# Expert layer of a two-block network on one core: a fourth weight buffer, sums of the dense part kept in `h`, gathered sums in the tile of `x`, gate tiles in another pool, stores on ScalarE's queue

## The chip, the cores and the metric

The kernel runs on one core of a Trainium2 chip. The metric is the device time of one execution in microseconds, as the median of several runs. The change concerns the expert layer (called `peer` in the code), but two of its edits resize buffer pools that all layers share.

## What is computed

A block with a hybrid mixer and an expert layer, then a second block with a pooling layer and a sparse attention layer, on 256 tokens of width 2048. The expert layer picks, for every token, 8 heads x 16 experts out of 16384, and each expert is one row of `expert_down` and one of `expert_up`:

```python
def block(args):
    xb, idx, gb = args
    u = expert_down[idx]
    act = jax.nn.gelu(jnp.einsum('thkd,td->thk', u, xb), approximate=False)
    vv = expert_up[idx]
    return jnp.einsum('thk,thkd->td', (gb * act).astype(vv.dtype), vv)
```

## The kernel before

**Weights.** Every large matrix comes in tiles of 1 MB (128 x 2048 fp32). `split_w` (L149) takes a buffer `wr` from a pool of three, lets SyncE (SP) issue the load, and then splits each half of the tile: ScalarE rounds it to `wh` (L159), VectorE subtracts to get the rest `wl` (L161). TensorE multiplies with both parts. A buffer `wr` is free again when the second `wl` has been made; SP issues the load into it at that time, in the order of its own queue. The weights of the second block's modulation (`in_mod_w`, L1008) use the same three buffers and are worked on by VectorE alone (L1014).

**The expert layer does tokens in two ways.** Tokens 0 to 191 go through all 16384 experts densely: 128 weight tiles of `in_down`, the activation (GELU), a multiplication with a table of gates that is zero for experts that were not picked, and 128 weight tiles of `in_up`. Tokens 192 to 255 go by gathers: GpSimd (POOL) fetches, slot by slot, the 128 rows (1 MB) that the 64 tokens need, by an indirect DMA into a tile `fm` (L772); VectorE multiplies and sums such a row tile with the tile of `x` (`x2`, L780) for `down_rows`, and multiplies it with the slot's activation and adds it to `acc` (L795) for `up_rows`. There are 64 gathers for each. `fm` has seven buffers, of which three hold the packed input `hx` of the dense part.

**Order.** The code runs over 16 panels of experts. `down(c)` takes four tiles and `up(p)` eight. The first 18 `down` stand alone; then `up` of a panel and two `down` take turns, and the last `up` stand alone. Results of the first seven panels (`LAG = 7`) are stored to DRAM (`hidden`, L843) and loaded again in `prep` (L856). `step()` is called after each weight tile and advances the gathers by `PUMP = 0.57`. The list scheduler that comes after the recording decides each engine's order from priorities and from buffers that it sees as free, so pools move work.

**Gate table.** `gate_table` builds, in 24 blocks, the gates of 8 tokens at a time out of one-hot tiles `A`, `B` in pool `s4` (L746, VectorE), multiplies them on TensorE (L732), collects 16 tokens in a tile of pool `gl` (L735, ScalarE) and stores it to DRAM (L738, SP). `prep` loads the gates of a panel into one `fm` tile (L860), multiplies (L865) and splits the result (L868, L869).

**Pool `gl`** has six buffers of 8 KB per partition. In the expert layer it holds `x2`, the sums `acc` of `up` for tokens 128 to 191 (their hi parts in partitions 0 to 63, their lo parts in 64 to 127, folded at the end by a product with `ff`, L897), the gathered sums `acc` (L785), activations and the split operands of `up`. `h` holds the 256 tokens' stream in two halves of 128 partitions; the rows 64 to 127 of its second half are the 64 gathered tokens.

Of the kernel before, what the change touches and what calls it, by code (L numbers as in the profile page):

```python
# [10 lines left out]
F32 = mybir.dt.float32  # L11
# [11 lines left out]
D = 2048  # L23
# [14 lines left out]
class Kern:  # L38
    def __init__(self, tc, ctx, d):
        self.tc, self.nc, self.d = tc, tc.nc, d  # L40
        pool = lambda name, bufs, **kw: ctx.enter_context(tc.tile_pool(name=name, bufs=bufs, **kw))
        self.cst = self.ph = pool("cst", 1)
        self.wr = pool("wr", 3)
        self.whp = pool("wh", 3)
        self.wlp = pool("wl", 3)
        self.fmp = pool("fm", 7)
        self.gl = pool("gl", 6)
        self.s4 = pool("s4", 4)
        self.s2 = pool("s2", 4)
        self.sm = pool("sm", 2)  # L50
        self.k1 = pool("k1", 4)
        self.mdp = pool("md", 1)
        self.accp = pool("acc", 4, space=PSUM)
        self.trp = pool("tr", 2, space=PSUM)
        self.msp = pool("ms", 2, space=PSUM)
        self.cnt = 0
        self.consts()
        self.mods = self.mod_steps()
        self.posts, self.seq, self.bg_rate, self.bg_due, self.nmods = [], [], 0.0, 0.0, 0
        self.pump, self.credit = None, 0.0  # L60
# [650 lines left out]
    def gate_table(self, R, G):  # L711
# [11 lines left out]
        def products(n, A, B):  # L723
# [13 lines left out]
            if n % GT == GT - 8:  # L737
                nc.sync.dma_start(G[n // GT], st)  # L738

# [13 lines left out]

    def gathers(self, h, R, inv, x2, ff):

# [28 lines left out]
        nc.vector.tensor_tensor(act, act, gt, op=OP.mult)  # L784
        acc = self.t_gl([128, D])  # L785
        for j in range(66):
            if j < 64:
                issue("up_rows", j)
            if j >= 2:
                r = rows.pop(j - 2)  # L790
                c = act[:, j - 2:j - 1]
                if j == 2:
                    nc.vector.tensor_scalar(acc, r, c, None, op0=OP.mult)
                else:
                    nc.vector.scalar_tensor_tensor(acc, r, c, acc, op0=OP.mult, op1=OP.add)  # L795
            yield
        for dc in range(4):
            cs = slice(dc * 512, (dc + 1) * 512)
            p = self.p_ms()
            nc.tensor.matmul(p, ff[:, 0:128], acc[:, cs], start=True, stop=True)  # L800
            nc.vector.tensor_tensor(h[:, 1, cs], h[:, 1, cs], p, op=OP.add)
            yield

    def peer(self, h):
# [18 lines left out]
        S = self.tc.dram_tile([LAG, 128, 8, TD], F32, name="hidden")  # L823
        C, act = {}, {}

        def down_post(c, tm):
# [15 lines left out]
            if i < LAG:  # L842
                nc.sync.dma_start(S[i, :, 4 * q:4 * q + 4], dst)  # L843

# [8 lines left out]
        def prep(p):  # L853
# [3 lines left out]
            else:  # L857
                a = act.pop(p)
            g8 = self.t_fm([128, TD // GT, 8, GT], F32)
            nc.sync.dma_start(g8, G[:, :, 8 * p:8 * p + 8, :].rearrange("g p i t -> p g i t"))  # L860
            c0, cp = self.t_gl([128, 2, 8, 128], F32R), self.t_s4([128, 8, 128], F32R)
            for q in range(2):
                s = slice(4 * q, 4 * q + 4)
                a4 = a[:, s].rearrange("p i (g t) -> p g i t", t=GT)
                nc.vector.tensor_tensor(a4, a4, g8[:, :, s], op=OP.mult)  # L865
                for hi, lo, src in ((c0[:, 0, s], c0[:, 1, s], a[:, s, 0:128]),
                                    (cp[:, s, 0:64], cp[:, s, 64:128], a[:, s, 128:TD])):
                    nc.scalar.activation(hi, src, AF.Copy)  # L868
                    nc.vector.tensor_tensor(lo, src, hi.bitcast(F32), op=OP.subtract)  # L869
            C[p] = c0, cp  # L870

        ss = self.ss_mod(0)
        acc = None
        ups = [*range(LAG, 15), 0, 15, *range(1, LAG)]

        def up(p):
            nonlocal acc
            if p == ups[0]:
                acc = self.t_gl([128, D])
            c0, cp = C.pop(p)  # L880
            xs = [(c0[:, 0, e], c0[:, 1, e], cp[:, e]) for e in range(8)]
            for dc in range(4):
# [5 lines left out]
                with self.first(end):  # L888
                    s = h[:, 0, cs]
                    nc.vector.tensor_tensor(s, s, ps[0], op=OP.add)  # L890
                    if p == ups[0]:
                        nc.vector.tensor_copy(acc[:, cs], ps[1])
                    else:
                        nc.vector.tensor_tensor(acc[:, cs], acc[:, cs], ps[1], op=OP.add)
                    if p == ups[-1]:
                        q = self.p_ms()
                        nc.tensor.matmul(q, ff[:, 64:192], acc[:, cs], start=True, stop=True)  # L897
                        nc.vector.tensor_tensor(h[:, 1, cs], h[:, 1, cs], q, op=OP.add)
                        for t in range(2):
# [13 lines left out]
        for c in range(4):  # L913
# [6 lines left out]
            if c == 0:  # L920
                nc.vector.scalar_tensor_tensor(x2[64:128], h[64:128, 1], inv[64:128, 1:2], x2[64:128],
                                               op0=OP.mult, op1=OP.mult)
                nc.scalar.dma_start(x2[0:64], x2[64:128])

        def start():
            yield
            self.pump = self.gathers(h, R, inv, x2, ff)
            next(self.pump)
# [574 lines left out]
```

## Time and profile before

| what | value |
|---|---|
| time, three runs | 2772.51, 2777.41, 2774.01 us |
| median | 2774.01 us |
| profiled execution, its own time | 2777.65 us |
| its span on the core | 2775.9 us |
| granted TensorE clock, mean | 0.983 |
| busy: TensorE 2642.5, VectorE 2244.1, ScalarE 1394.2, GpSimd 271.3 us | 95%, 81%, 50%, 10% of the span |
| read from HBM, written | 759.11 MB, 20.23 MB |

The profile is of one execution, whose own time is 3.6 us above the median and 1.75 us longer than its span. Matmuls overlap, so a share of busy time near 100% does not mean that TensorE is at its peak; how many matmuls it ran in a stretch tells more. "DMA share" is the mean busy share of the core's 16 DMA engines. The chain that ended last is followed back from the last instruction and says, for each piece of time, which work the end was waiting for.

### The profile page before, as it was taken

The numbers are of one execution on the slowest core, as the hardware profiler recorded it, in microseconds if no ns is written. First come the engines' busy times: TensorE is split into PE (matmuls) and PEld (weight loads), VectorE is DVE, ScalarE is ACT, GpSimd is POOL, SyncE is SP. The second block draws the span as 40 slices with busy tenths as digits, with TensorE's granted clock in tenths as the row PEclk, the third lists the DMA queues.
The fourth block names the chain that finished last, engine by engine and source line by source line (L and its number), as shares of the span: only waits on it lengthen the run. The fifth ranks groups of instructions, "written<-read, shape, count | busy, mean of one in ns | idle before, by whom it ended". The sixth has DMA issues, their size and how long they took to land.

```text
span 2775.9 us, 33244 instructions
## 1 busy us (share of the span) xinstructions
PE 2642.5 (95%) x12296; PEld 2142.0 (77%) x12296; DVE 2244.1 (81%) x3162; ACT 1394.2 (50%) x1881; POOL 271.3 (10%) x210
## 2 busy tenths in 40 slices
PE   8999999998998999999999899998999799999998
PEld 6787778877876777787877677777887687888886
DVE  6988886999997898768998789967779867765655
ACT  5547555554654444454544444444444444455543
POOL 1000000001112222102322212000000000000000
PEclk9999999999999999999999999999999899999999
DMA  7666675557999999869999999765788855655554
GB/s 291 261 224 227 259 261 203 195 202 265 382 374 398 358 372 373 320 238 334 406 366 374 353 363 357 291 224 219 277 304 324 310 201 193 226 208 187 182 194 170
DMA packets 135123, 782.08 MB, mean 282 GB/s; under 512 B 14000, under 2 KB 38736, under 8 KB 43760
## 3 DMA queue, kind: packets, MB, share of 16 engines
q1 hardware_dynamic: 113680, 639.81, 62.4%
q0 software_dynamic: 20752, 138.53, 12.8%
q8 instruction: 96, 1.57, 0.2%
q10 hardware_dynamic: 528, 1.61, 0.2%
q14 instruction: 67, 0.55, 0.1%
HBM read 759.11 MB, written 20.23 MB: 281 GB/s over the span
## 4 chain that ended last, share of the span: by engine, by line
PE 64%; DVE 14%; DMA 13%; issue 4%; ACT 3%; POOL 0%; ACTq 0%; DVEq 0%; POOLq 0%; SPq 0%
PE acc L170 16%; PE acc L171 16%; PE acc L169 16%; DVE wl L161 6%; PE acc L219 5%; PE acc L220 5%; DMA wr<-in_down 4%; DMA wr<-in_up 4%; ACT wh L159 2%; DMA wr<-in_mod_w 2%; DVE md L1014 1%; PE tr L267 1%; DVE gl L795 1%; DVE fm L780 1%; DMA wr<-in_pool_w_out 1%
## 5 line engine op out<-in xcount | busy, mean ns | idle before, releaser
L159 ACT ACTIVATE wh<-wr 128x1024 fp32r<-128x1024 f32 x944 | 991.4, 1058 | 1127.1 <-PE acc L171 380.7
L161 DVE TENSOR_TENSOR wl<-wr,wh 128x1024 fp32r<-128x1024 f32 x944 | 1140.5, 1220 | 408.2 <-ACT wh L159 398.9
L170 PE MATMUL acc<-wl,fm 128*128 128x512 f32 x1952 | 775.0, 397 | 29.5 <-DVE wl L161 28.7
L169 PE MATMUL acc<-wh,fm 128*128 128x512 f32 x1952 | 780.6, 402 | 16.4 <-ACT wh L159 14.4
L171 PE MATMUL acc<-wh,fm 128*128 128x512 f32 x1952 | 768.3, 394 | 0.0
L170 PEld LDWEIGHTS acc<-wl,fm 128*128 128x128 f32 x1952 | 370.5, 190 | 124.1 <-DVE wl L161 50.7
L169 PEld LDWEIGHTS acc<-wh,fm 128*128 128x128 f32 x1952 | 369.5, 190 | 95.5 <-ACT wh L159 18.8
L171 PEld LDWEIGHTS acc<-wh,fm 128*128 128x128 f32 x1952 | 370.1, 190 | 75.0
L170 PE MATMUL acc<-wl,gl 128*128 128x512 f32 x768 | 307.9, 401 | 18.6 <-DVE wl L161 18.6
L169 PE MATMUL acc<-wh,gl 128*128 128x512 f32 x768 | 305.2, 398 | 10.6 <-ACT wh L159 9.4
L171 PE MATMUL acc<-wh,gl 128*128 128x512 f32 x768 | 302.6, 394 | 0.0
L1014 DVE SCALAR_TENSOR_TENSOR md<-wr,c_c,md 128x1024 f32<-128x1024 f32 x180 | 230.4, 1280 | 35.4 <-DMA wr<-in_mod_w 33.4
L219 PE MATMUL acc<-wh,s 128*128 128x512 f32 x512 | 202.8, 396 | 0.0
L220 PE MATMUL acc<-wl,s 128*128 128x512 f32 x512 | 202.7, 396 | 0.0
L219 PE MATMUL acc<-wh,fm 128*128 128x512 f32 x512 | 202.2, 395 | 0.0
L220 PE MATMUL acc<-wl,fm 128*128 128x512 f32 x512 | 202.0, 395 | 0.0
L170 PEld LDWEIGHTS acc<-wl,gl 128*128 128x128 f32 x768 | 145.2, 189 | 63.9 <-DVE wl L161 31.8
L169 PEld LDWEIGHTS acc<-wh,gl 128*128 128x128 f32 x768 | 145.0, 189 | 46.0 <-ACT wh L159 12.2
L772 POOL DMA_INDIRECT fm<-in_up_rows,slot_rows x64 | 124.0, 1938 | 482.1 <-DVE gl L795 257.0
L171 PEld LDWEIGHTS acc<-wh,gl 128*128 128x128 f32 x768 | 145.5, 189 | 31.7 <-issue 1.0
L795 DVE SCALAR_TENSOR_TENSOR gl<-fm,slot_act,gl 128x2048 f32<-128x2048 f32 x63 | 147.7, 2344 | 6.1 <-DMA fm<-in_up_rows,slot_rows 6.1
L780 DVE SCALAR_TENSOR_TENSOR fm<-fm,gl 128x2048 f32<-128x2048 f32 x64 | 146.1, 2284 | 0.2 <-DMA fm<-in_down_rows,slot_rows 0.2
(416 smaller groups left out, 2377.6 us busy)
## 6 DMA issues: line engine op xcount, KB each, us to landing
wr<-in_down SPq DMA_DIRECT2D x128, 1024.0 KB, 8.6
wr<-in_up SPq DMA_DIRECT2D x128, 1024.0 KB, 8.1
wr<-in_mod_w SPq DMA_DIRECT2D x96, 1024.0 KB, 5.2
wr<-in_attn_w_in SPq DMA_DIRECT2D x72, 1024.0 KB, 4.8
wr<-in_w_in SPq DMA_DIRECT2D x44, 1024.0 KB, 5.2
wr<-in_pool_w_in SPq DMA_DIRECT2D x32, 1024.0 KB, 5.3
wr<-in_w_out SPq DMA_DIRECT2D x16, 1024.0 KB, 4.8
wr<-in_peer_query SPq DMA_DIRECT2D x16, 1024.0 KB, 4.7
```

Source lines behind the costliest of these rows:

```text
L159: nc.scalar.activation(wh, wr[:, s], AF.Copy)
L161: nc.vector.tensor_tensor(wl, wr[:, s], wh.bitcast(F32), op=OP.subtract)
L169: mm(ps, xl, wh, start=first, stop=False)
L170: mm(ps, xh, wl, start=False, stop=False)
L171: mm(ps, xh, wh, start=False, stop=last)
L219: mm(ps[1], xp, h, start=st, stop=False)
L220: mm(ps[1], xp, l, start=False, stop=sp)
L267: self.nc.tensor.transpose(p[:, j, t * 128:(t + 1) * 128], src(t, k + j), self.ident)
L772: nc.gpsimd.indirect_dma_start(rows[j], None, d[src], bass.IndirectOffsetOnAxis(ap=ei[:, j:j + 1], axis=0))
L780: nc.vector.scalar_tensor_tensor(r, r, 1.0, x2, op0=OP.mult, op1=OP.mult, accum_out=act[:, j - 2:j - 1])
L795: nc.vector.scalar_tensor_tensor(acc, r, c, acc, op0=OP.mult, op1=OP.add)
L1014: nc.vector.scalar_tensor_tensor(acc, w[:, j], cd[:, k:k + 1], acc, op0=OP.mult, op1=OP.add)
```

## The change

- Pool `wr` gets four buffers in place of three; pool `gl` five in place of six.
- The second sum of `up` goes into `h[:, 1]` itself. For that, rows 64 to 127 of `h[:, 1]` (the gathered tokens) are stored to a DRAM tile `h_last` early on and set to zero, and at the end they are loaded into a `gl` tile `last`, whose other half is zero; the gathered sums are added to `last`, and the fold adds `last` too. The separate `gl` tile for the sum of `up` is gone.
- The gathered sums of `up_rows` go into `x2`, which is no longer needed once the last `down_rows` has been multiplied.
- The gates of a panel come by two DMAs into two `s4` tiles, in place of one DMA into one `fm` tile.
- The stores of the gate table and of `hidden` are issued by ScalarE (ACT) and not by SP.

```diff
-        self.wr = pool("wr", 3)
+        self.wr = pool("wr", 4)
...
-        self.gl = pool("gl", 6)
+        self.gl = pool("gl", 5)
...
             if n % GT == GT - 8:
-                nc.sync.dma_start(G[n // GT], st)
+                nc.scalar.dma_start(G[n // GT], st)
...
-    def gathers(self, h, R, inv, x2, ff):
+    def gathers(self, R, x2, ff, last):
...
-        acc = self.t_gl([128, D])
+        acc = x2
...
+        last.append(self.t_gl([128, D]))
+        nc.gpsimd.memset(last[0][0:64], 0.0)
+        nc.sync.dma_start(last[0][64:128], self.h_last)
         for dc in range(4):
...
             nc.tensor.matmul(p, ff[:, 0:128], acc[:, cs], start=True, stop=True)
-            nc.vector.tensor_tensor(h[:, 1, cs], h[:, 1, cs], p, op=OP.add)
+            nc.vector.tensor_tensor(last[0][:, cs], last[0][:, cs], p, op=OP.add)
...
             if i < LAG:
-                nc.sync.dma_start(S[i, :, 4 * q:4 * q + 4], dst)
+                nc.scalar.dma_start(S[i, :, 4 * q:4 * q + 4], dst)
...
-            g8 = self.t_fm([128, TD // GT, 8, GT], F32)
-            nc.sync.dma_start(g8, G[:, :, 8 * p:8 * p + 8, :].rearrange("g p i t -> p g i t"))
+            g8 = [self.t_s4([128, TD // GT, 4, GT]) for _ in range(2)]
+            for q in range(2):
+                i = 8 * p + 4 * q
+                nc.sync.dma_start(g8[q], G[:, :, i:i + 4, :].rearrange("g p i t -> p g i t"))
...
-                nc.vector.tensor_tensor(a4, a4, g8[:, :, s], op=OP.mult)
+                nc.vector.tensor_tensor(a4, a4, g8[q], op=OP.mult)
...
-                    s = h[:, 0, cs]
-                    nc.vector.tensor_tensor(s, s, ps[0], op=OP.add)
-                    if p == ups[0]:
-                        nc.vector.tensor_copy(acc[:, cs], ps[1])
-                    else:
-                        nc.vector.tensor_tensor(acc[:, cs], acc[:, cs], ps[1], op=OP.add)
+                    for t in range(2):
+                        s = h[:, t, cs]
+                        nc.vector.tensor_tensor(s, s, ps[t], op=OP.add)
                     if p == ups[-1]:
                         q = self.p_ms()
-                        nc.tensor.matmul(q, ff[:, 64:192], acc[:, cs], start=True, stop=True)
-                        nc.vector.tensor_tensor(h[:, 1, cs], h[:, 1, cs], q, op=OP.add)
+                        nc.tensor.matmul(q, ff[:, 64:192], h[:, 1, cs], start=True, stop=True)
+                        nc.vector.tensor_tensor(h[:, 1, cs], last[0][:, cs], q, op=OP.add)
...
                 nc.scalar.dma_start(x2[0:64], x2[64:128])
+                nc.scalar.dma_start(self.h_last, h[64:128, 1])
+                nc.gpsimd.memset(h[64:128, 1], 0.0)
```

The order of instructions moves at two places that matter here. The first is SP's queue where the gate table is made. Before, stores (`hidden`, `gates`) stand between the loads of weights:

```order
L154 DMA wr_5937<-in_down 128x2048
L843 DMA hidden<-s_1096_5626 128x768
L154 DMA wr_6000<-in_down 128x2048
L154 DMA wr_6060<-in_down 128x2048
L843 DMA hidden<-s_1138_5836 128x768
L738 DMA gates<-gl_5782 128x2048
L154 DMA wr_6134<-in_down 128x2048
```

Of the change, SP has nothing but loads of weights there, 48 of `in_down` in a row, and the two kinds of store stand in ScalarE's queue, behind the activations that write their tiles:

```order
L159 ACTIVATE wh_5942<-wr_5940 128x1024
L845 ACTIVATE s_1138_5839<-tr_5840 128x384
L845 ACTIVATE s_1138_5839<-tr_5846 128x384
L735 ACTIVATE gl_5785<-ms_5859 128x128x4
L847 DMA hidden<-s_1138_5839 128x768
L735 ACTIVATE gl_5785<-ms_5869 128x128x4
L738 DMA gates<-gl_5785 128x2048
L159 ACTIVATE wh_5946<-wr_5940 128x1024
```

So 26 stores left SP's queue for ScalarE's.

The second place is VectorE's order about the 122nd to 124th of the expert layer's 256 weight tiles, between the last gather of `down_rows` and the first of `up_rows` of the kernel before. There VectorE has only the splits of weights, the sums of `up` (`h` and the tile `gl_8164`) and a panel's gates:

```order
L161 TENSOR_TENSOR wl_9935<-wr_9927,wh_9933 128x1024
L161 TENSOR_TENSOR wl_9980<-wr_9976,wh_9978 128x1024
L161 TENSOR_TENSOR wl_9984<-wr_9976,wh_9982 128x1024
L890 TENSOR_TENSOR h<-h,acc_9895 128x512
L894 TENSOR_TENSOR gl_8164<-gl_8164,acc_9896 128x512
L161 TENSOR_TENSOR wl_10013<-wr_10009,wh_10011 128x1024
L865 TENSOR_TENSOR gl_9812<-gl_9812,fm_10175 128x12x4x16
L161 TENSOR_TENSOR wl_10017<-wr_10009,wh_10015 128x1024
```

Of the change, the gathered rows of `up_rows` (`fm`, L795) are already being added there, into the tile of `x2` (`gl_3640`), both sums of `up` go to `h`, and the gates come from an `s4` tile:

```order
L795 SCALAR_TENSOR_TENSOR gl_3640<-fm_11168,slot_act,gl_3640 128x2048
L161 TENSOR_TENSOR wl_9941<-wr_9937,wh_9939 128x1024
L161 TENSOR_TENSOR wl_9945<-wr_9937,wh_9943 128x1024
L161 TENSOR_TENSOR wl_9990<-wr_9986,wh_9988 128x1024
L795 SCALAR_TENSOR_TENSOR gl_3640<-fm_11235,slot_act,gl_3640 128x2048
L161 TENSOR_TENSOR wl_9994<-wr_9986,wh_9992 128x1024
L161 TENSOR_TENSOR wl_10023<-wr_10019,wh_10021 128x1024
L893 TENSOR_TENSOR h<-h,acc_9905 128x512
L893 TENSOR_TENSOR h<-h,acc_9906 128x512
L871 TENSOR_TENSOR gl_9822<-gl_9822,s_1981_10186 128x12x4x16
L161 TENSOR_TENSOR wl_10027<-wr_10019,wh_10025 128x1024
```

So the second series of gathers starts at about the 111th weight tile in place of the 135th. Counted in VectorE's order between the same weight tiles, its 64 rows stand as follows.

| weight tiles of the expert layer | `up_rows` before | `up_rows` of the change |
|---|---|---|
| 104 to 135 | 2 | 21 |
| 136 to 183 | 35 | 37 |
| 184 to 231 | 22 | 6 |
| 232 to 255 | 5 | 0 |

The 64 rows of `down_rows` keep their places up to tile 103 but for one.

## Rows read from the trace of the kernel before

**Rows 1.** The page, part 4: the chain that ended last, shares by engine.
```profile
PE 64%; DVE 14%; DMA 13%; issue 4%; ACT 3%; POOL 0%; ACTq 0%; DVEq 0%; POOLq 0%; SPq 0%
```

**Rows 2.** Windows of the expert layer: length, busy and instructions of PE, PEld, DVE, ACT, POOL.
```profile
core 0: us, PE busy (x) PEld busy (x) DVE busy (x) ACT busy (x) POOL busy (x), PEclk, DMA share, GB/s
...
649.00:804.00 155.00, 145.92 (x917) 119.09 (x915) 147.32 (x203) 88.86 (x122) 25.69 (x17) 0.96 0.92 355
804.00:1119.00 315.00, 285.46 (x1289) 225.56 (x1288) 268.69 (x255) 145.40 (x173) 75.58 (x47) 0.99 0.96 374
1119.00:1270.00 151.00, 149.49 (x669) 122.33 (x670) 106.50 (x104) 75.25 (x84) 10.02 (x6) 0.99 0.76 276
1270.00:1514.00 244.00, 234.07 (x1038) 187.27 (x1037) 222.49 (x187) 117.91 (x134) 66.04 (x33) 0.99 0.97 376
1514.00:1763.00 249.00, 232.72 (x981) 183.67 (x979) 217.87 (x214) 116.20 (x131) 50.84 (x28) 0.97 0.93 357
1763.00:1881.00 118.00, 117.86 (x499) 93.56 (x500) 93.53 (x92) 54.32 (x61) 1.17 (x2) 1.00 0.66 236
```

**Rows 3.** The same windows, instructions with `wl` alone: DVE makes two per weight tile.
```profile
804.00:1119.00 315.00, 182.19 (x455) 85.89 (x454) 134.28 (x112) 0.99 0.96 374
1119.00:1270.00 151.00, 98.51 (x249) 47.27 (x249) 77.72 (x64) 0.99 0.76 276
1270.00:1514.00 244.00, 153.13 (x386) 72.72 (x386) 114.68 (x97) 0.99 0.97 376
1514.00:1763.00 249.00, 154.97 (x387) 73.35 (x386) 115.15 (x97) 0.97 0.93 357
```

**Rows 4.** The chain that ended last, 804 to 1119 us, by line.
```profile
by line: DMA wr<-in_down 31.3%; DVE wl L161 11.5%; DVE fm L780 9.1%; issue 8.4%; DMA wr<-in_up 5.8%; PE acc L170 4.4%; DMA fm<-gates 4.4%; PE acc L220 3.9%; PE acc L171 3.9%; PE acc L219 3.9%; ACT wh L159 3.7%; PE acc L169 3.6%; DMA wr<-in_
```

**Rows 5.** DMA, 804 to 1119 us, in 40 equal slices.
```profile
GB/s 333 354 383 347 426 419 424 419 314 418 423 377 231 334 376 384 416 420 370 274 401 410 290 373 356 307 408 423 420 379 359 382 399 393 383 305 390 382 366 375
```

**Rows 6.** Timeline of POOL, 1100 to 1280 us: start, duration, instruction, idle before.
```profile
1141.98 1.97 POOL L772 DMA_INDIRECT fm<-in_up_rows,slot_rows  x1 [0.31 <-issue]
1210.83 0.93 POOL L772 DMA_INDIRECT fm<-in_up_rows,slot_rows  x1 [66.88 <-DVE gl L865]
1265.40 0.94 POOL L772 DMA_INDIRECT fm<-in_up_rows,slot_rows  x1 [53.64 <-DVE gl L793]
```

**Rows 7.** VectorE's gathered rows: L780 from 804 to 1119 us; L795 by windows.
```profile
L780 DVE SCALAR_TENSOR_TENSOR fm<-fm,gl 128x2048 f32<-128x2048 f32 x49 | 111.9, 2284 | 0.2 <-DMA fm<-in_down_rows,slot_rows 0.2
...
1119.00:1270.00 151.00, 2.34 (x1) 0.99 0.76 276
1270.00:1514.00 244.00, 82.08 (x35) 0.99 0.97 376
1514.00:1763.00 249.00, 51.57 (x22) 0.97 0.93 357
1763.00:1881.00 118.00, 11.70 (x5) 1.00 0.66 236
```

**Rows 8.** Waits of SP's queue, whole span: total us, times, longest.
```profile
SPq L843 <- ACT s L841: 39.8, 11, 7.9
...
SPq L860 <- DVE gl L795: 31.9, 9, 6.0
...
SPq L738 <- ACT gl L735: 28.1, 11, 5.7
```

**Rows 9.** VectorE's groups, 649 to 804 us: busy, mean ns, idle before.
```profile
L746 DVE TENSOR_TENSOR s<-s,slot_major 128x1024 f16<-128x1024 f16 x45 | 29.3, 684 | 5.0 <-DMA hidden<-s 5.0
```

**Rows 10.** The first 70 us: SP's timeline, and a wait of PE.
```profile
28.68 2.27 SPq L297 DMA_DIRECT2D h<-in_x  x2
...
PE acc L169 <- ACT wh L159: 9.6, 2, 9.2
```

**Rows 11.** The whole span's DMA issues: KB each, median us from issue to landing.
```profile
fm<-gates SPq DMA_DIRECT2D x16, 768.0 KB, 8.8
...
gl<-hidden SPq DMA_DIRECT2D x7, 768.0 KB, 6.5
```

**Rows 12.** A DMA that ScalarE issues in the kernel before: duration in ns.
```profile
L923 ACTq DMA_DIRECT2D gl<-gl x1: 519/519/519, 438.0 to 438.0; - x1
```

More of the change, by code (lines that the diff above doesn't have):

```diff
@@ L823, in peer @@
         S = self.tc.dram_tile([LAG, 128, 8, TD], F32, name="hidden")
-        C, act = {}, {}
+        self.h_last = self.tc.dram_tile([64, D], F32, name="h_last")
+        C, act, last = {}, {}, []
         def down_post(c, tm):
@@ L872, in peer @@
         ss = self.ss_mod(0)
-        acc = None
         ups = [*range(LAG, 15), 0, 15, *range(1, LAG)]
         def up(p):
-            nonlocal acc
-            if p == ups[0]:
-                acc = self.t_gl([128, D])
             c0, cp = C.pop(p)
@@ L888, in up @@
                 with self.first(end):
-                    s = h[:, 0, cs]
-                    nc.vector.tensor_tensor(s, s, ps[0], op=OP.add)
-                    if p == ups[0]:
-                        nc.vector.tensor_copy(acc[:, cs], ps[1])
-                    else:
-                        nc.vector.tensor_tensor(acc[:, cs], acc[:, cs], ps[1], op=OP.add)
+                    for t in range(2):
+                        s = h[:, t, cs]
+                        nc.vector.tensor_tensor(s, s, ps[t], op=OP.add)
                     if p == ups[-1]:
                         q = self.p_ms()
-                        nc.tensor.matmul(q, ff[:, 64:192], acc[:, cs], start=True, stop=True)
-                        nc.vector.tensor_tensor(h[:, 1, cs], h[:, 1, cs], q, op=OP.add)
+                        nc.tensor.matmul(q, ff[:, 64:192], h[:, 1, cs], start=True, stop=True)
+                        nc.vector.tensor_tensor(h[:, 1, cs], last[0][:, cs], q, op=OP.add)
                         for t in range(2):
@@ L923, in peer @@
                 nc.scalar.dma_start(x2[0:64], x2[64:128])
+                nc.scalar.dma_start(self.h_last, h[64:128, 1])
+                nc.gpsimd.memset(h[64:128, 1], 0.0)
         def start():
             yield
-            self.pump = self.gathers(h, R, inv, x2, ff)
+            self.pump = self.gathers(R, x2, ff, last)
             next(self.pump)
```

## The prediction, made before the changed kernel ran

> **What bounds the kernel now.** I read the chain of waits first: 64% of the span it runs through TensorE, 13% through DMA, 14% through VectorE [rows 1], so TensorE sets the pace except where weights come late. Where that is, the windows of the expert layer tell [rows 2]. I call them T (649 to 804 us), S1 (804 to 1119), S2 (to 1270), S3 (to 1514), S4 (to 1763) and S5 (to 1881). In S2 TensorE is busy for 149.5 of 151 us and runs 669 instructions, one in 0.226 us; I take this as its full rate. VectorE makes two `wl` per weight tile [rows 3], and a tile needs 20 matmuls in this layer, so S1, with 112 `wl`, is 56 tiles and 1120 matmuls: 253 us at full rate. Its other 169 instructions are short transposes and products of 128 columns or fewer, at half the time or less, some 17 us. TensorE needs 270 us of the 315; the rest, some 45 us, is the largest loss of the layer. By the same count S3 (48.5 tiles, 68 others) needs 226 of 244 and S4 (11 others) 220 of 249.
>
> In S1 the chain runs for 31.3% through loads of `in_down` and 5.8% through loads of `in_up` [rows 4]: a buffer is freed, the load is issued, it lands, it is split. So S1 waits for weights. The reader is to see beside it that the DMA engines are not at rest there: share 0.96, 374 GB/s [rows 2], in single slices of 8 us between 231 and 426 [rows 5], with about a third of the slices above 405. VectorE is busy for 269 of 315 us. In S2 by contrast TensorE is the bound, DMA share is 0.76 and VectorE has 44 us free. The reason stands in POOL's timeline: GpSimd sat idle for 66.9 and then 53.6 us, with one gather between [rows 6]. First it waited for an `fm` tile that held gates, then for the first row to be multiplied (L793), which had no `gl` tile for `acc`. The gathers that S2 didn't make lie in S3 and S4.
>
> **The change part by part.**
>
> *Fourth buffer.* It lets a fourth load be under way while three are landing or being split. S1 keeps its work (its rows of L780 [rows 7] keep their places but for one), so its gain is bounded by the resource next to full. DMA: 374 GB/s x 315 us = 117.8 MB, at 420 GB/s, the better slices, 280 us; VectorE 269, TensorE 270. So from 0 to 35 us. Slices of low rate are partly those with small packets and stores, which a buffer doesn't speed up; I take 14.
>
> *No gap between the gathers.* In the instruction order the windows' tiles get 19 more rows in S2, 2 more in S3, 16 fewer in S4 and 5 fewer in S5. A row is a DMA of 1.05 MB and 2.35 us of VectorE (82.08/35, [rows 7]), of which some 5% overlaps its neighbours, so 2.23.
> S2: DMA 276 x 151 = 41.7 MB plus 19.9 = 61.6 MB, at 420 GB/s 147 us, at 374 GB/s 165; VectorE 106.5 + 42.4 = 149; TensorE 149.5. Three resources meet at 150 and won't interleave perfectly; I take 160, so 9 us slower, with 0 and 24 as bounds (24: the ratio of span to VectorE's busy time that S1 shows, 315/268.7 = 1.17, times 149).
> S3: 91.7 + 2.1 = 93.8 MB, at 420 GB/s 223, at 374 GB/s 251; VectorE 227, TensorE 226. With the fourth buffer 243 in place of 244; bounds 226 and 266 (again 1.17 x 227).
> S4: 357 x 249 = 88.9 MB less 16.8 leaves 72 MB, 171 us at 420 GB/s; VectorE 217.9 - 35.7 = 182. Neither binds any more, TensorE's 220 does. The first 16 tiles still have all 6 rows and four panels' gates, so 228: 21 us faster, bounds 10 and 29.
> S5: 499 instructions at the full rate are 113 us of the 118, and five rows leave: 1 us, bounds 0 and 5.
>
> *Stores on ScalarE's queue.* SP stood 39.8 us behind `hidden` and 28.1 behind `gates` [rows 8] with weights queued behind it, and in T one `hidden` store that landed late held VectorE for 5.0 us [rows 9], since its `s4` tile was wanted for a one-hot tile. VectorE is busy for 147 of T's 155 us, so T can give at most 8; I take 4. The price is 26 issues on ScalarE, each at most 0.52 us [rows 12], 13.5 us in all. ScalarE's own work (145 of 315 us in S1) hides them; a store waits only for activations just ahead of it in the same queue. If the cover were gone, the next `wh` would be half a microsecond late, and TensorE holds one and a half split tiles against that.
>
> *Gates in `s4`.* Gates no longer take an `fm` tile: SP loses the 31.9 us behind L795 [rows 8] and the gathers have four tiles all the time. Instead there are 32 loads with runs of 256 bytes for 16 with runs of 512, and in the last panels they wait on SP until the `up` two panels back has released its operands, with weights behind them. In SP's order such a load stands four or five tiles ahead of what it waits for, as far as the weights themselves run ahead with four buffers, so I count nothing for that wait. For the smaller runs: 768 KB of gates land in 8.8 us, 768 KB of `hidden` in 6.5 [rows 11], so runs of 512 bytes cost up to 2.3 us more than long ones; halving them might cost nothing or as much again, 1 us as my estimate. DMA binds only for the nine or so panels of S1 to S3: between 0 and 21 us of DMA time, of which half is hidden where VectorE or TensorE binds as well; I take 3, bounds 0 and 9.
> The Trainium skill's "DMA: Bandwidth & Descriptors", section "Specifications", asks for at least 512 bytes per transfer for line rate, which speaks against this edit. No row here shows loads of 256-byte runs in number. By that rule the 12.6 MB of gates would go at about half the rate and cost some 2 us per panel, an estimate from that page, inside the bounds just given.
>
> *The rest.* At the start `h` is loaded only at 28.7 us, queued behind weights that wait for buffers, and TensorE waits 9.2 us for a `wh` that stands on ScalarE behind the norm of `h` [rows 10]. The fourth buffer moves that load ahead by one tile, about 4 us: I take 3, bounds 0 and 5. The saved rows of `h` (0.5 MB out and in), two clears on GpSimd and the sums into `h` add nothing to the path: GpSimd is idle, the DMA load falls before the gathers and in S4/S5, and VectorE makes one sum for each that it made before. `gl` with five: in the instruction order the first writes of `gl` tiles in mixer, pooling and attention stand where they stood, within a tile or two; I count nothing. If one chunk's destination did come late, it would hold four tiles of 24 matmuls, 22 us.
>
> **Sum.** -14 + 9 - 1 - 21 - 1 - 4 + 3 - 3 = -32 us against the profiled 2777.65, which gives 2746 for such an execution. The median of the runs lies 3.6 us below it, so 2742.
>
> **Rivals.**
> *Slower.* S2 and S3 become one stretch of 395 us in which VectorE, DMA and TensorE are all nearly full, and each waits for the other two as in S1: at S1's ratio of 1.17, S2 costs 24 and S3 22 us more, and the fourth buffer gains nothing in S1. Then 24 + 22 - 21 - 1 + 3 - 4 - 3 = +20, 2794. For it speaks S1; against it the 244 us of S3 for 222 of VectorE (1.10) with three buffers. It decides once S2 and S3 together pass 421 us with S1 unchanged, or 435 with S1 as I have it. Chance 0.15.
> *No change.* The DMA rate is the bound in S1 and S3 and 374 GB/s is all it gives, so more outstanding loads only wait longer: S1 0, S2 +14, S3 +7, S4 -21, S5 -1, packets +3, T and start nothing: +2, 2776. For it: share 0.96. Against it: the slices above 405 GB/s. Chance 0.15.
> The same page and section of the Trainium skill puts the HBM limit of a core at about 358 GB/s; by that rule S1 and S3 are already beyond their limit and this rival would hold, with 2776. The 374 GB/s of a whole window and slices up to 426 [rows 2, 5] disagree.
> *All of it.* Every stretch falls to the bound of its fullest resource: 35 + 0 + 18 + 29 + 5 + 8 + 5 = 100 us, 2674. Chance 0.07; the way there holds the rest of my low side.
>
> **How the numbers follow.** My forecast (2710 to 2768) has 0.63. A difference of 0.2%, 5.5 us, is about what a measurement of this kernel can tell from no change. Forecast and "all of it" are faster, 0.70; no change 0.15; slower 0.15. The range takes in no change and the edge of slower: 2710 to 2782. Below lie "all of it" and part of its way, above most of "slower". Without the cases of other sign the range would be 2710 to 2768.
>
> **What the profile would show.** POOL's two long idle times gone. The last L795 at about 804 - 7 + 301 + 160 + 243 + 16 tiles x 4.7 = 1576 us, where it is at 1514 or later for 27 of 63 rows now. S1 with the same 49 rows of L780 in about 301 us, the chain's share of `in_down` there lower, the rate above 385 GB/s. S2's tiles in about 160 us with DMA share near 0.95; S4's in 228 with share below 0.75. No store on SP. I am wrong if S1 doesn't shorten (then DMA was the bound), if S2 and S3 pass 421 us, or if TensorE waits in S4 for weights behind a gates load.

## The result, and the profile after

| | before | after |
|---|---|---|
| median, same chip | 2775.71 us (2772.51 to 2778.06, 4 runs) | 2730.74 us (2721.41 to 2733.91, 4 runs) |
| ratio | | 0.9834, 95% interval 0.9815 to 0.9853 |
| profiled execution, span | 2775.9 us | 2719.6 us |

The change makes the kernel 45 us faster; forecast were 32. The profiled execution of after is its fastest, 9 us below the median, so its stretches add up to 56 us. A second profile of the same kernel, taken later with the experiments, adds up to 48 and has the same stretches within 3 us. I cut the trace at the same weight tiles as in [rows 2].

Windows of the expert layer after the change, T, S1, S2, S3, S4, S5 in this order:

```profile
core 0: us, PE busy (x) PEld busy (x) DVE busy (x) ACT busy (x) POOL busy (x), PEclk, DMA share, GB/s
644.00:799.00 155.00, 145.75 (x922) 118.30 (x921) 147.56 (x203) 88.83 (x122) 23.42 (x17) 0.97 0.92 354
799.00:1096.00 297.00, 279.11 (x1280) 225.79 (x1279) 266.56 (x255) 145.57 (x171) 78.00 (x48) 0.98 1.01 398
1096.00:1249.00 153.00, 152.17 (x683) 124.21 (x682) 149.62 (x127) 78.80 (x89) 46.51 (x25) 0.99 1.02 402
1249.00:1478.00 229.00, 227.81 (x1030) 186.35 (x1029) 222.76 (x183) 117.54 (x131) 70.48 (x38) 1.00 1.01 400
1478.00:1712.00 234.00, 226.17 (x977) 183.30 (x976) 186.88 (x200) 116.10 (x131) 4.65 (x6) 0.98 0.87 294
1712.00:1831.00 119.00, 119.00 (x507) 94.69 (x506) 83.02 (x86) 55.31 (x63) 2.35 (x2) 1.00 0.68 238
```

Against [rows 2] three stretches are shorter: S1 297 us for 315, S3 229 for 244, S4 234 for 249. S2, in which GpSimd now works instead of resting, takes 153 for 151. T and S5 stay. DMA moves 398 to 402 GB/s through all of S1 to S3, where it moved 374, 276 and 376.

Chain over the whole span, by engine; it answers to [rows 1]:

```profile
PE 62%; DMA 6%; DVE 4%; issue 2%; ACT 1%; POOL 0%; ACTq 0%; POOLq 0%; DVEq 0%
```

DMA's share of it fell from 13 to 6%, VectorE's from 14 to 4%. Inside S1 (the chain that ended last, 799 to 1096 us, by line):

```profile
by line: DMA wr<-in_down 18.8%; DMA wr<-in_up 15.8%; PE acc L170 9.3%; PE acc L171 8.8%; PE acc L220 8.7%; PE acc L219 8.7%; PE acc L169 8.5%; DVE wl L161 5.9%; DMA wr<-in_mod_w 3.8%; issue 3.7%; DVE fm L780 2.9%; ACT wh L159 2.7%; ACT s L8
```

Loads of weights still hold 34.6% of S1's chain (37.1% in [rows 4]), but `wl`, L780 and the gates have left it to matmuls.

POOL's timeline about the start of S2; columns as in [rows 6]:

```profile
1083.81 1.68 POOL L772 DMA_INDIRECT fm<-in_down_rows,slot_rows  x1 [3.94 <-DVE fm L780]
1100.60 1.68 POOL L772 DMA_INDIRECT fm<-in_up_rows,slot_rows  x1 [15.10 <-DVE fm L780]
...
1127.31 1.68 POOL L772 DMA_INDIRECT fm<-in_up_rows,slot_rows  x1 [8.10 <-DVE gl L793]
1133.05 1.68 POOL L772 DMA_INDIRECT fm<-in_up_rows,slot_rows  x1 [4.05 <-DVE gl L795]
```

The two idle times of 66.9 and 53.6 us are gone; the longest here is 15.1. The last multiply of a gathered row (L795) starts at 1556.7 us (1795.1 before; 1576 was forecast):

```profile
L795 DVE SCALAR_TENSOR_TENSOR gl<-fm,slot_act,gl x63: 2334/2344/2347, 1130.4 to 1556.7; 128x2048 f32<-128x2048 f32 x63
```

SP's waits over the whole span have a new entry in place of those of [rows 8], and in T the wait of [rows 9] is still there (VectorE's group, busy, mean ns, idle before):

```profile
SPq L866 <- DVE gl L871: 59.1, 20, 11.6
```
```profile
L746 DVE TENSOR_TENSOR s<-s,slot_major 128x1024 f16<-128x1024 f16 x46 | 30.1, 683 | 4.5 <-DMA hidden<-s 4.5
```

### The profile page after: what moved, and what is told of

It is laid out like the page before. It is cut to its first block, busy times and chain, and to the rows that moved or that the text cites. A ratio compares the mean times of both kernels' runs of the same rounds, so it can differ in the third digit from the quotient of the medians.

```text
span 2719.6 us, 33286 instructions
## 1 busy us (share of the span) xinstructions
PE 2616.1 (96%) x12296; PEld 2141.0 (79%) x12296; DVE 2240.6 (82%) x3162; ACT 1402.9 (52%) x1883; POOL 272.0 (10%) x212
## 4 chain that ended last, share of the span: by engine, by line
PE 62%; DMA 6%; DVE 4%; issue 2%; ACT 1%; POOL 0%; ACTq 0%; POOLq 0%; DVEq 0%
PE acc L170 15%; PE acc L169 15%; PE acc L171 15%; PE acc L220 7%; PE acc L219 7%; DMA wr<-in_down 2%; DVE wl L161 2%; DMA wr<-in_up 2%; DMA wr<-in_mod_w 2%; PE tr L267 1%; PE ms L732 1%; DMA gl<-hidden 1%; ACT wh L159 1%; DVE md L1015 1%; PE tr L844 0%
## 5 line engine op out<-in xcount | busy, mean ns | idle before, releaser
L795 DVE SCALAR_TENSOR_TENSOR gl<-fm,slot_act,gl 128x2048 f32<-128x2048 f32 x63 | 147.6, 2344 | 0.0
L780 DVE SCALAR_TENSOR_TENSOR fm<-fm,gl 128x2048 f32<-128x2048 f32 x64 | 146.0, 2281 | 0.0
```

What stands on the lines that cost most here:

```text
L780: nc.vector.scalar_tensor_tensor(r, r, 1.0, x2, op0=OP.mult, op1=OP.mult, accum_out=act[:, j - 2:j - 1])
```

## The experiments

Three theories stood at the start. *Buffer theory*: the fourth weight buffer gives most of it. *Gap theory*: the gathers that moved from S3 and S4 into S2 do. *Queue theory*: the stores that left SP do. The ratios are against the kernel before on the same chip. To compare small differences I also give the length of the layer from T to S5, which is 1232 us before and 1187 after (1190 in the second profile of after), since it is free of what the first 500 us do.

**e1_three: after, with three weight buffers.**

```diff
-        self.wr = pool("wr", 4)
+        self.wr = pool("wr", 3)
```

> The changed kernel with three weight buffers in place of four, all else as changed; VectorE's order of gathered rows is that of the changed kernel within a row or two. Buffer theory (the gain is loads that can start one tile earlier, so that the DMA engines have no gaps): S1, the 56 tiles with the rows of L780, goes back from 297 to about 315 us, S2 and S3 with their 58 dense rows lose 15 or more, the start loses 4; S4 keeps its 15; in all about 2765 (2758 to 2775). Gap theory (the gain is the gathers that fill the empty stretch S2 and leave S4): the buffer is minor, 2735 to 2745. Queue theory (the gain is SP rid of stores and of waits for gates): 2735 to 2745 too, with S1 near 300.

Measured: 2767.89 us, ratio 0.9971 (0.9954 to 0.9988); layer 1233 us. S1 to S4 of it:

```profile
807.10:1116.00 308.90, 285.81 (x1257) 229.09 (x1257) 265.42 (x251) 146.36 (x173) 75.91 (x48) 0.96 0.98 380
1116.00:1283.40 167.40, 155.83 (x672) 122.94 (x673) 150.13 (x125) 75.51 (x86) 43.69 (x25) 0.98 0.96 366
1283.40:1530.00 246.60, 234.37 (x1034) 187.13 (x1034) 224.24 (x185) 116.09 (x130) 69.30 (x38) 0.99 0.97 373
1530.00:1759.30 229.30, 224.97 (x975) 182.60 (x974) 184.78 (x199) 115.95 (x130) 3.29 (x5) 0.99 0.86 295
```

Without the fourth buffer all other edits together are worth 8 us. S4 is short by them, but S2 (167 us in place of 151) and T (162 in place of 155) pay it back, and DMA runs at 366 to 380 GB/s in S1 to S3. In S2 this is two thirds of what the rival "slower" described (24 us); the 22 us that it had for S3 did not come.

**e2_alone: before, with four weight buffers** (and five of `gl`).

```diff
-        self.wr = pool("wr", 3)
+        self.wr = pool("wr", 4)
...
-        self.gl = pool("gl", 6)
+        self.gl = pool("gl", 5)
```

> The kernel before with four weight buffers and five of pool gl, nothing else; the gap between the two series of gathers stays, stores and gates stay on SP and in fm. Buffer theory: S1 about 300 us, S3 and S4 a few us shorter, start 4 shorter: about 2745 (2738 to 2755). Gap theory: 2765 to 2775. Queue theory: 2770 or more, since SP still stands behind stores and gates.

Measured: 2744.38 us, ratio 0.9892 (0.9854 to 0.993); layer 1214 us. The buffer alone is worth 32 us by the medians; the profiles show 18 in the layer. S1, S3 and S4:

```profile
799.50:1099.30 299.80, 279.21 (x1283) 227.25 (x1283) 266.46 (x255) 146.45 (x171) 78.14 (x46) 0.98 0.98 390
...
1252.00:1494.30 242.30, 232.99 (x1036) 189.07 (x1035) 222.80 (x187) 119.17 (x134) 62.87 (x33) 0.99 0.98 379
1494.30:1738.90 244.60, 229.83 (x974) 185.03 (x973) 222.64 (x211) 114.17 (x124) 58.68 (x29) 0.96 0.95 359
```

S1 has nearly all its gain here (315 to 300), S3 and S4 have little of theirs (244 to 242, 249 to 245).

**e3_acc: after, with the gathered sums in a `gl` tile again**, so that the gap of [rows 6] comes back, and the gathers to S3 and S4.

```diff
-        acc = x2
+        acc = self.t_gl([128, D])
```

> The changed kernel with the gathered sums in a gl tile of their own again; VectorE's order then has the gap between the series back (2 rows of up_rows up to tile 135, 35 to 183 as before the change). Buffer theory: S1 stays at 297, S2 at 150, S3 about 235, S4 about 235: 2732 to 2745, so no gap costs little once there are four buffers. Gap theory: 2755 to 2770.

Measured: 2733.07 us, ratio 0.9854 (0.9806 to 0.9903); layer 1191 us. S1 to S4:

```profile
808.70:1105.20 296.50, 278.63 (x1279) 225.74 (x1278) 266.18 (x255) 145.35 (x171) 77.25 (x48) 0.98 1.01 399
1105.20:1256.70 151.50, 151.32 (x681) 123.85 (x680) 107.68 (x105) 77.85 (x87) 10.11 (x6) 0.99 0.79 280
1256.70:1493.50 236.80, 232.94 (x1050) 189.63 (x1048) 223.06 (x185) 118.89 (x133) 70.26 (x39) 1.00 1.00 391
1493.50:1724.80 231.30, 225.28 (x959) 182.21 (x960) 217.66 (x213) 115.16 (x128) 37.77 (x22) 0.97 1.01 376
```

S2 rests as before (10 us of POOL), S4 has its gathers (VectorE 217.7 us) and takes 231 us all the same. So the gap theory falls: filling the gap is worth 1 to 4 us of the layer, hardly more than the 3 us by which two profiles of after differ. What e2_alone lacks in S3 and S4 and e3_acc has is the gates in `s4`, the sums of `up` in `h`, which leave one more `gl` tile free, or the stores (for which see the next run): 23 us of the layer, 11 of the medians. The first two were not run apart with the gap. The sums in `h` are a rival: in e2_alone SP stands 17.9 us behind the `gl` tile that a load of `hidden` wants, and e3_acc has no such wait. From e2_alone:

```profile
SPq L856 <- DVE gl L869: 17.9, 6, 4.4
```

**e4_sp: after, with the 26 stores on SP.**

```diff
-                nc.scalar.dma_start(G[n // GT], st)
+                nc.sync.dma_start(G[n // GT], st)
...
-                nc.scalar.dma_start(S[i, :, 4 * q:4 * q + 4], dst)
+                nc.sync.dma_start(S[i, :, 4 * q:4 * q + 4], dst)
```

> The changed kernel with the 26 stores of gates and hidden issued by SP again. Buffer and gap theory: within 5 us of the changed kernel, since the stretch T (gate table) took 155 us on either queue and VectorE still waited 4.5 us for a hidden store. Queue theory: 8 us or more slower, in T and in the first tiles of S1.

Measured: 2730.12 us, ratio 0.9838 (0.9803 to 0.9873); layer 1190 us, T 154.8. The queue theory falls: the stores' queue makes no difference. In T the stores of `hidden` land as soon from SP as from ScalarE (DMA issues in T, KB each, median us to landing; of after, then of this run):

```profile
gates<-gl ACTq DMA_DIRECT2D x11, 1024.0 KB, 9.4
hidden<-s ACTq DMA_DIRECT2D x7, 384.0 KB, 7.7
```
```profile
gates<-gl SPq DMA_DIRECT2D x11, 1024.0 KB, 8.8
hidden<-s SPq DMA_DIRECT2D x7, 384.0 KB, 7.6
```

**e5_fm: after, with the gates in an `fm` tile again.** It tells whether the gates' pool is what was left, or their short runs.

```diff
-            g8 = [self.t_s4([128, TD // GT, 4, GT]) for _ in range(2)]
-            for q in range(2):
-                i = 8 * p + 4 * q
-                nc.sync.dma_start(g8[q], G[:, :, i:i + 4, :]...)
+            g8 = self.t_fm([128, TD // GT, 8, GT], F32)
+            nc.sync.dma_start(g8, G[:, :, 8 * p:8 * p + 8, :]...)
```

> The changed kernel with the gates of a panel loaded again as one tile of fm (runs of 512 bytes), all else kept. Tile theory: a gates tile that sits in fm for its panel takes one of four buffers from the gathers and puts SP behind a multiply of a gathered row, with weights queued behind; that is what the kernel with only the fourth buffer still lost in the stretches of tiles 136 to 231 (242.3 and 244.6 us, where the changed kernel had 229 and 234). Then this kernel comes out at 2740 to 2746, with those two stretches together above 475 us and the time 2.5 to 3 per cent of it no better than with the buffer alone. Packet theory: runs of 256 bytes cost DMA time where DMA is full, so 512 gives back 1 to 2 us for each of the panels of tiles 48 to 135: 2715 to 2724, with the first stretch below 292 us. Neither: within 4 us of 2731.

Measured: 2776.08 us, ratio 1.0009 (0.9997 to 1.0021); layer 1233 us. The whole gain is gone; the tile theory names the right cause, but 30 us too little of it, and the packet theory falls. S3, then waits (total us, times, longest): of VectorE in the layer, of GpSimd in S2 and S3, and of TensorE in the layer, the last for this run and for after:

```profile
1269.30:1533.10 263.80, 240.35 (x1032) 193.59 (x1031) 188.74 (x169) 118.00 (x131) 29.09 (x18) 0.95 0.77 288
```
```profile
DVE gl L795 <- DMA fm<-in_up_rows,slot_rows: 56.2, 21, 7.9
POOL fm L772 <- DVE gl L869: 58.8, 3, 36.2
PE acc L170 <- DVE wl L161: 62.8, 34, 11.7
```
```profile
PE acc L170 <- DVE wl L161: 22.9, 15, 7.8
```

In S3 no resource is full: DMA share 0.77, VectorE 189 of 264 us. VectorE stands 56.2 us, in 21 waits, before gathered rows that haven't landed, with the `wl` of weights queued behind; in after this line has no wait at all, in before 6.1 us. With a gates tile in it `fm` has three free buffers, and the gathers come later than the place that VectorE's order gives to their multiplies: three times GpSimd waits, 58.8 us in all, until the gates have been multiplied (L869 here). TensorE pays at the end of this row of waits: 40 us more behind `wl` than in after. In S3 it stands still for 23.5 us, and its 1032 instructions take 240 us at a granted clock of 0.95, where after's 1030 take 228 at 1.00.

**e6_pin64, e6_pin57: the gathers spread evenly.** In after, S1 still takes 297 us, where TensorE needs 270 by the prediction's count, with a DMA share of 1.01. If DMA is the bound, fewer gathers there should help. The multiplies of gathered rows keep their place in the program, and the pump's rate is 0.64 or 0.57.

```diff
-PUMP = 0.57
+PUMP = 0.64
...
-                nc.vector.scalar_tensor_tensor(r, r, 1.0, x2, ...)
+                self.tc.keep_in_program_order(nc.vector.scalar_tensor_tensor(r, r, 1.0, x2, ...))
...
-                    nc.vector.scalar_tensor_tensor(acc, r, c, acc, ...)
+                    self.tc.keep_in_program_order(nc.vector.scalar_tensor_tensor(acc, r, c, acc, ...))
```

> The changed kernel with the multiplies of gathered rows held to their place in the program, and the pump's rate at 0.64 in place of 0.57: the gathers then stand about 5 to each 8 weight tiles from tile 24 to tile 230, where the changed kernel has 7 in the first stretch (tiles 48 to 103), 6 up to tile 183 and then none. Nothing else is changed. DMA theory: with four buffers the first stretch is held by DMA alone (297 us at 398 GB/s, share 1.01); ten to twelve gathers fewer there are 11 MB, 28 us at 398 GB/s, until TensorE's 270 binds: the first stretch falls to 272 to 282, the others stay within 4 us, and the time is 2708 to 2718. Mixing theory: what holds the first stretch is not the bytes but that DMA, VectorE and TensorE wait for each other in turn; it stays above 290, and the last panels, which now carry gathers, lose 5 to 10 us: 2730 to 2742.

> The even order with the pump's rate as in the changed kernel (0.57): 4 to 5 gathers to each 8 tiles, the last at tile 255. DMA theory: the first stretch (tiles 48 to 103) has 34 gathers instead of 49 and is bound by TensorE at 270 to 278 us; nothing further is won over the rate 0.64, so 2706 to 2718; the last multiplies end with the layer and could hold its end by 1 to 3 us. Mixing theory: 2730 to 2745, and slower than the rate 0.64 because the tail is longer.

Measured: rate 0.64 2725.09 us, ratio 0.9812 (0.979 to 0.9834); rate 0.57 2712.72 us, ratio 0.9782 (0.9767 to 0.9797). Layer 1179 and 1178 us. The DMA theory holds at 0.57. At 0.64 it holds for S1 (282 us, its upper edge) and misses for S4, which takes 250 us with the gathers that it now has, and for the time, by 7 us. Since the two layers differ by 1 us in these profiles, the lead of 0.57 over 0.64 stays open.

**e6_pin64w3: the even order with three weight buffers** (the pool's line as in e1_three).

> The same even order of the gathers with three weight buffers instead of four. Buffer theory: a wait of one load chain is paid at each burst whatever the order, so the fourth buffer is still worth 25 to 40 us: 2740 to 2755. Order theory: three buffers were too few only because seven gathers per 8 tiles crowded the loads of the first stretch and six those after; with five per 8 tiles the third buffer's load lands in time, and the fourth is worth less than 12 us: 2712 to 2730.

Measured: 2753.7 us, ratio 0.9921 (0.9906 to 0.9935); layer 1212 us. The fourth buffer is worth 29 us in the even order too, as the buffer theory expects.

**e7_run128: after, with gates in runs of 128 bytes; e7_base and e7_even beside it**: after itself, and the even order at 0.57, on the same chip.

```diff
-                nc.sync.dma_start(g8[q], G[:, :, i:i + 4, :]...)
+                for k in range(0, 4, 2):
+                    nc.sync.dma_start(g8[q][:, :, k:k + 2], G[:, :, i + k:i + k + 2, :]...)
```

> The changed kernel with each load of gates split in two, so that the same bytes come in runs of 128 bytes instead of 256, in twice as many packets and 32 more issues on SP. Packet theory: small packets take DMA time where DMA is full; if 256-byte runs cost a panel 1 us or more against long ones (the prediction's +3 in all), halving them once more doubles that, and the first stretch (297 us), the second (153) and the third (229), all with a DMA share above 1.0, get longer by 10 us or more together: the time is 2738 to 2755. Free theory: the number of packets doesn't bind, since other transfers fill the engines between them; then the three stretches stay within 4 us together and the time is within 4 us of the changed kernel's.

> The changed kernel itself, beside the two others on one chip, as their base: all theories expect 2725 to 2735.

> The even order of gathers at the pump's rate 0.57 once more, beside the changed kernel on one chip. DMA theory: 10 to 20 us faster than the changed kernel, with the first stretch near 277 us against 297. Rival: its lead came from the chip on which it ran, and side by side the two are within 5 us.

Measured: e7_run128 2749.57 us, ratio 0.9921 (0.9903 to 0.994); e7_base 2729.05 us, 0.9849 (0.9827 to 0.9872); e7_even 2711.93 us, 0.9795 (0.977 to 0.982). S1 to S3 of e7_run128, then of e7_base:

```profile
809.00:1117.00 308.00, 282.12 (x1268) 226.84 (x1267) 266.24 (x254) 146.23 (x172) 75.61 (x48) 0.97 1.01 383
1117.00:1272.00 155.00, 152.24 (x679) 123.54 (x678) 148.38 (x125) 77.76 (x89) 51.79 (x25) 0.99 1.01 393
1272.00:1508.00 236.00, 229.77 (x1032) 186.43 (x1031) 222.16 (x184) 117.47 (x132) 83.47 (x38) 1.00 1.02 390
```
```profile
802.00:1101.00 299.00, 280.89 (x1267) 227.34 (x1265) 266.97 (x254) 146.39 (x172) 75.65 (x48) 0.98 1.01 395
1101.00:1254.00 153.00, 152.21 (x683) 124.35 (x682) 149.16 (x126) 78.48 (x89) 46.74 (x25) 0.99 1.01 402
1254.00:1483.00 229.00, 227.82 (x1031) 186.61 (x1029) 222.62 (x184) 117.89 (x130) 76.37 (x38) 1.00 1.01 399
```

With the same DMA share (1.01 to 1.02), 9 to 12 GB/s fewer get through, and the three stretches are 9 + 2 + 7 = 18 us longer: packets are paid for where DMA is full. The even order's S1 and S4:

```profile
800.00:1074.00 274.00, 273.73 (x1285) 225.66 (x1284) 238.19 (x227) 147.28 (x172) 53.66 (x33) 1.00 0.99 377
...
1454.00:1695.00 241.00, 229.13 (x974) 182.75 (x973) 224.61 (x208) 113.52 (x124) 51.00 (x32) 0.99 1.01 380
```

S1 takes 274 us, 25 fewer than e7_base, and TensorE is busy for all of them; S4 and S5, which now have gathers, give 15 back. On one chip the even order is 17 us faster than the changed kernel (2711.93 for 2729.05), and the slowest of its five runs, 2724.61, is below the fastest of e7_base, 2726.53. This is the fastest kernel of the study.

**e8_run512: after, with gates in runs of 512 bytes**, still in two `s4` tiles, split by tokens.

```diff
-            g8 = [self.t_s4([128, TD // GT, 4, GT]) for _ in range(2)]
+            g8 = [self.t_s4([128, hg, 8, GT]) for _ in range(2)]
...
-                nc.sync.dma_start(g8[q], G[:, :, i:i + 4, :]...)
+                nc.sync.dma_start(g8[q], G[q * hg:(q + 1) * hg, :, 8 * p:8 * p + 8, :]...)
...
-                nc.vector.tensor_tensor(a4, a4, g8[q], op=OP.mult)
+                nc.vector.tensor_tensor(a8, a8, g8[q], op=OP.mult)
```

> The changed kernel with the two gates tiles of a panel split by tokens instead of by columns: the same two tiles of the same pool and the same bytes, now in runs of 512 bytes and half as many packets (some 24,600 fewer). The two multiplies by the gates have the same size, but each covers half the tokens of all eight columns, so the split into high and low parts begins after both. Packet theory: 128-byte runs cost some 20 us for 49,000 more packets; by the same price 24,600 fewer give back up to 10 us, in the stretches where DMA is full: 2718 to 2725. Knee theory: only runs below 256 bytes take longer than their bytes, so 512 gives back nothing: 2726 to 2734. Against both, the later start of the split could cost TensorE 1 to 2 us for a panel that is late already: 2735 to 2745.

Measured: 2727.36 us, ratio 0.9835 (0.9817 to 0.9854); layer 1189 us. S1 to S3 take 296 + 155 + 228 = 679 us, against 681 in e7_base and 679 in the first profile of after. So the knee theory has the time right, but DMA's own time speaks against it. The queue that carries weights and gates, from S1 to S3, for runs of 512, 256 (e7_base) and 128 bytes (e7_run128): packets, MB, the time that its packets took, as a share of the 16 engines' time in the three stretches (679.0, 680.6 and 698.8 us):

```profile
q1 hardware_dynamic: 34265, 153.82, 57.4%
q1 hardware_dynamic: 48082, 153.79, 58.6%
q1 hardware_dynamic: 76028, 153.87, 60.1%
```

That is 390, 399 and 420 us for the same bytes. The step from 512 to 256 costs 9 us for 13,800 packets, the step to 128 costs 21 us for 28,000: nearly the same price per packet, so no knee. Only the second step shows in the layer's time. Why the first doesn't is not shown: in this run the split also begins later, which may have taken back what DMA gave.

## Why the prediction was right, and where its terms were off

| stretch | before, us | forecast change | after | where it came from |
|---|---|---|---|---|
| T | 155 | -4 | 0 | |
| S1 | 315 | -14 | -18 | buffer -15 (e2_alone) |
| S2 | 151 | +9 | +2 | gap filled: +1.5 (against e3_acc) |
| S3 | 244 | -1 | -15 | buffer -2, gates' pool or sums in `h` -5, gap -8 |
| S4 | 249 | -21 | -15 | buffer -4, gates' pool or sums in `h` -13, gap +3 |
| S5 | 118 | -1 | +1 | |
| packets | (S1 to S3) | +3 | 0 | 9 us of DMA's time, none of the layer's (e8_run512) |
| start | 649.0 | -3 | -5 | not told from the clock, see the last section |
| after the layer | 894.9 | 0 | -6 | seen with four buffers only |

The column "after" gives changes too, from the first profile.

**The number: in part luck.** Of the two parts that make up the sum, the fourth buffer in S1 came as forecast (-14; -15 in e2_alone), and the filled gap (+9 - 1 - 21 - 1 = -14 in S2 to S5) was worth 4 us at most. In its place came a gain for which the sum had no term, from the gates' pool (with the gap, perhaps in part from the sums in `h`). The two errors have opposite signs, and so the total stayed near.

**Fourth buffer: right.** It holds S1's gain, and without it nothing else pays (e1_three). The prediction kept DMA's 374 GB/s from being a limit by the slices above 405 of [rows 5]; after runs at 398 to 402 GB/s from S1 to S3. So the rival "no change" fell. The Trainium skill's "DMA: Bandwidth & Descriptors", section "Specifications", puts a core's HBM limit at about 358 GB/s, a stack's rate halved between two cores; this kernel, which runs on one core, moved over 10% more. The buffer's term was low in two places: I gave it next to nothing in S3 and S4, and nothing after the layer. After the layer four-buffer kernels take 886.6 to 893.6 us and three-buffer kernels 894.9 to 896.0. The two groups don't overlap, but two executions of the even order differ by 6 us there, and which wait went wasn't taken apart.

**No gap: the term that failed in its mechanism.** The forecast gave S4 -21 because its gathers leave, and S2 +9 because three resources meet. Both were wrong. S4 is as short with all its gathers (e3_acc, 231 us), and S2 fits 149.6 us of VectorE and 152.2 of TensorE into 153 us at a DMA share of 1.02. With four buffers each of the three can be nearly full at the same time; with three they can't (167 us, e1_three). So filling the gap was worth 4 us at most, and the rival "slower" needed three buffers. The place of the gathers does matter elsewhere: with 15 of them taken out of S1, where DMA is full, the even order is 17 us faster than the changed kernel.

**Gates in `s4`: the term that was missing.** I priced this edit as a cost (+3). I named its relief of `fm`, SP's wait behind L795 [rows 8] and a fourth tile for the gathers, and gave it no term. Where the gap stays, it and the sums in `h` together are worth 23 us of the layer (e2_alone against e3_acc); with the gap filled it decides everything (e5_fm, 45 us slower than after). The cause that e5_fm's trace shows is VectorE waiting in order for rows whose gathers waited for a gates tile's buffer. In before that wait was only 6.1 us, and in e2_alone, with the gap and four weight buffers, 11.6, so its row did not announce it: it grew when the gap was filled.

**Short runs: right in DMA's time.** By the same page and section of the Trainium skill, transfers under 512 bytes fall below line rate. The traces agree in direction: 256-byte runs take 9 us more of DMA's time than 512-byte runs. For the nine panels of S1 to S3 that is the 1 us per panel that the prediction read from [rows 11], and half of the 2 us that it worked out from the page. Of the layer's time it cost nothing that can be measured here, while 128-byte runs (with 32 more issues on SP) cost 18 us. S4's DMA share is 0.87, where below 0.75 was forecast: short runs are a part of it, for it is 0.92 with 128 bytes and 0.83 with 512.

**SP's wait for gates: rightly left out.** SP stands behind the multiplies by gates for 59.1 us in all, and S4's matmuls still fill 226 of 234 us. What S4 lacks lies behind a load of `hidden`, not of gates: it took 17.4 us to land, and VectorE waited for it with `wl` behind it in its queue (from the chain of after, then VectorE's wait, 1478 to 1529 us):

```profile
1471.91 17.38 DMA gl<-hidden
```
```profile
DVE gl L871 <- DMA gl<-hidden: 9.8, 1, 9.8
```

Other four-buffer kernels have one such load at the start of S4 too: of gates in e3_acc (18.6 us), of `in_mod_w` in e6_pin64 (15.5 us), of `in_up` in e7_even (12.0 us).

**Stores: failed.** T did not shorten, because the store that `s4` waits for lands no sooner on ScalarE's queue (7.7 us, from SP 7.6), so VectorE still waits 4.5 us (4.9 in e4_sp). Their 26 issues cost nothing either.

**All of it, 2674:** not reached, but the even order goes a third of the way from after (2712), with S1 at TensorE's bound.

## What to carry to other kernels

A full pipeline's missing overlap shows as "share 0.96, nothing quite full": here one more buffer for what streams was worth more (29 to 37 us) than any order of the gathers that was tried (17 us). Before two kinds of tiles share a pool, ask which in-order engine would stand behind a late one; a wait that is small in a trace may grow when another stall is taken away. Once DMA share passes 1.0 in a stretch and another stretch has room, move transfers between them.

## What was not expected of the hardware

The first 500 us differ between executions of one kernel. The even order was profiled twice, with spans of 2724.4 and 2709.6 us; its layer takes 1178 and 1177 us, and 8 of the 15 us lie before T. Windows at two places there (columns as in [rows 2]), of the slower execution and then of the faster:

```profile
130.00:135.00 5.00, 4.26 (x19) 3.89 (x20) 5.00 (x11) 0.54 (x2) 0.56 (x1) 0.57 0.75 298
160.00:165.00 5.00, 2.34 (x12) 1.49 (x10) 5.00 (x11) 1.60 (x4) 0.00 (x0) 0.98 0.77 301
165.00:170.00 5.00, 4.78 (x18) 4.20 (x18) 3.52 (x7) 0.76 (x3) 0.00 (x0) 0.50 0.61 215
```
```profile
130.00:135.00 5.00, 4.86 (x33) 4.04 (x34) 5.00 (x11) 2.68 (x6) 0.56 (x1) 1.00 0.59 237
160.00:165.00 5.00, 3.92 (x25) 3.27 (x24) 4.81 (x8) 2.76 (x6) 0.00 (x0) 1.00 0.65 241
165.00:170.00 5.00, 5.00 (x30) 4.26 (x29) 3.83 (x5) 2.08 (x4) 0.00 (x0) 1.00 0.34 107
```

In the slower one TensorE is busy for 2.34 of 5 us and is then granted 0.50, the lower of its two levels (1.2 GHz), and runs 18 instructions where the faster one runs 30. From 130 to 170 us its mean granted clock is 0.85. The profiles of e3_acc, e6_pin64 and e7_run128 have such a start too (0.85 or 0.86; T begins at 652.7 to 653.7 us), those of before, after and the others less of it or none (0.91 to 1.00; 644.0 to 650.0 us). So a term of 3 us at the start can't be told from this, nor can medians of four runs decide 5 us; the layer's length can. By the granted clock alone I can't say why one execution falls and the other does not.

DMA held 398 to 402 GB/s over 680 us, with a busy share just above 1.
